# Up products whose right operand holds both parts of the rows side by side, and converted weights made three ahead

## The chip, the core and the metric

The kernel runs on one core of one Trainium2 chip. The metric is the device time of one execution in microseconds (us). The core has a matrix engine (TensorE, PE in the profile, with its weight loads listed apart as PEld), three engines for elementwise work (VectorE or DVE, ScalarE or ACT, GpSimd or POOL), a queue engine (SyncE or SP) and 16 DMA engines. Each engine works through its own list of instructions in the order of the program. Where an instruction needs something of another engine it waits for a semaphore, and what stands behind it on its engine waits too.

## The reference

One decoder block over 512 rows of 2048 channels: RWKV-7 time mixing and sliding-window attention side by side, merged by gates, and then a gated feed-forward part. All values are float32. The change lies in the feed-forward part:

```python
def conv_ffn(h, w_up, conv_w, conv_b, w_down):
    u = h @ w_up                       # (512, 2048) @ (2048, 11264)
    up = jnp.pad(u, ((0, 0), (CONV_W - 1, 0), (0, 0)))
    c = up[:, 0:S] * conv_w[0] + up[:, 1:S + 1] * conv_w[1] + up[:, 2:S + 2] * conv_w[2] + conv_b
    val, gate = jnp.split(c, 2, axis=-1)
    return (jax.nn.silu(gate) * val) @ w_down
```

`h` is the block's state after an RMS norm. `u` is 512 rows by 2 x 5632 columns, the value half and the gate half.

## The kernel before

**Parts.** TensorE multiplies operands of type float32r. To keep the precision of float32, each factor is split into a high part (`hi`, the value rounded to float32r) and a low part (`lo`, what is left). A product is then the sum of three: high weights by high rows, high weights by low rows, low weights by high rows. ScalarE makes the high part with a copy (`act.activation(hi, t, AF.Copy)`), and VectorE makes the low part with a subtraction that reads the high part, so the low part always comes second.

**Stages.** The program runs through the input projection, time mixing, attention and the branch projection (to about 1315 us), the output projection (stage "o", line 997, to about 1470 us), the up projection (line 1133, 1472 to 2374 us) and the down projection (stage "dn", line 997 again, to the end).

**The up stage.** There are 44 blocks `f`, each of 128 value columns and the 128 gate columns that go with them. A block is multiplied by a scheme of seven products in place of eight: the two halves of the contraction, the two halves of the rows (256 each, `TH`) and the two column halves make 2 x 2 matrices, and the sums and differences of the factors are multiplied. The products are named P1, P2, P7, P6, P5, Q4 and P3. The row factors (`b11`, `b21`, `b22`, `t1` to `t4`) are made once, each as two tiles for the high and the low part (`bq`). The weight factors come from memory, some of them with a sum that a DMA forms on the way (`s1`, `s3`), and P6 and P3 need one more sum on VectorE (`sums`, line 1109), which adds in place to the tile that P1 used.

A product is 8 steps `k` of the contraction, and a step is three matmuls of 256 columns (lines 1130 to 1134): `(whi, xh)`, `(whi, xl)`, `(wlo, xh)`. From block 7 on the order within a block is P7, P6, P2, P5, P1 of the next block, Q4, P3. P1, P6, P5 and P3 add up in one PSUM tile X, P7 and Q4 in a tile Y, P2 in a tile Z. Each of these tiles is a whole bank of 512 columns, of which only the left 256 are used.

**Order of the work around a product.** `run(i)` (line 1261) first calls `prep(i + 2)`, then the matmuls `mm`, then `out`, which moves results into the row buffer `u`. `prep(j)` (line 1246) makes the converted weights of step `j`: the sum on VectorE if the product is P6 or P3, then one piece of the convolution of an earlier block (`some_later(1)`), then the high part on ScalarE (line 1114) and the low part on VectorE (line 1116). Nearly every instruction of this stage is held in program order (`pin`). The converted weights `whi` and `wlo` have three buffers each (`hlD`, line 962).

**The convolution** of a block is queued after its P3 and taken piece by piece, one for each `prep`. Piece 0: ScalarE scales the gate half (line 1182), VectorE adds the next tap (line 1185). Piece 1: VectorE adds the last tap, ScalarE applies silu to it (line 1188). Pieces 2 and 3 do the same with the value half, without silu. Piece 4 multiplies the two halves on VectorE (line 1190). Pieces 5 and 6, in odd blocks alone, form the sums that the down stage needs (lines 893 to 897), and the results go out from ScalarE's queue when piece 0 of the next block is taken.

**Results into `u`** (`out`, lines 1157 to 1165): for P1, P6, P5 and P3 ScalarE copies X into a part of `u` (line 1161). For P5, VectorE then adds Y (line 1163), and for P2 and Q4 VectorE adds Z or Y (line 1165). That is three VectorE additions of 128 x 256 in a block.

Of the kernel before, what the change touches and what calls it, by code (L numbers as in the profile page):

```python
# [18 lines left out]
P = 128  # L19
S = 512  # L20
# [114 lines left out]
def block_kernel(ctx: ExitStack, tc: tile.TileContext, d: Dims, a: dict, out: bass.AP):  # L135
    nc = tc.nc
    act, dve, pool, pe, sync = nc.scalar, nc.vector, nc.gpsimd, nc.tensor, nc.sync
# [17 lines left out]
    NPRE = 4  # L155
# [725 lines left out]
    KH = NK // 2  # L881
# [134 lines left out]

    upx = ExitStack()
    bqp = upx.enter_context(tc.tile_pool(name="bqA", bufs=1, reuse_waits="tile"))
    bq = {n: [bqp.tile([P, KH, TH], F32R, name=f"{n}{i}") for i in range(2)] for n in ("b11", "b21")}
    hp = hps.enter_context(tc.tile_pool(name="hhlO", bufs=3, reuse_waits="tile"))  # L1020
    NCC = d.D // S
    ssp = tcp.tile([P, NT, NCC], F32, name="ssp")
# [49 lines left out]
            else:  # L1072
                put(act.activation(dst, src, AF.Copy, scale=g))

    def halves(t):
        return t.rearrange("p (a k) s -> p a (k s)", a=2)

    def high(n, q, pin=pin):
        pin(act.activation(halves(bq[n][0]), q, AF.Copy))

    def low(n, q, pin=pin):
        hi, lo = (halves(x) for x in bq[n])
        pin(dve.tensor_tensor(lo, q, hi.bitcast(F32), op=ALU.subtract))

    us = []
    dve.tensor_scalar(cw[:, 0:3, NF:], cw[:, 0:3, NF:], -1.0, None, op0=ALU.mult)

    class Block:

        def __init__(self, f):
            self.f, self.w, self.hl = f, {}, {}
            self.apart = 2 <= f < NPRE

        def load(self, n):
            f, w = self.f, self.w
# [20 lines left out]
        def mm(self, n):  # L1118
            if n == "P1":
                x = ups.tile([P, S], F32, name="X", tag="X")  # L1120
                self.X = x[:, :TH]
                self.Z = x[:, TH:] if self.f < NPRE else upy.tile([P, S], F32, name="Z", tag="Y")[:, :TH]
            if n == "P7":
                self.Y = upy.tile([P, S], F32, name="Y", tag="Y")[:, :TH]
# [4 lines left out]
            xh, xl = bq[{"P1": "b11", "P2": "b21", "P7": "t3", "P6": "t2", "P5": "t1", "Q4": "t4", "P3": "b22"}[n]]  # L1129
            for k in range(KH):  # L1130
                last = k == KH - 1
                for i, (l, r) in enumerate(((whi, xh), (whi, xl), (wlo, xh))):
                    pin(pe.matmul(ps, l[:, k], r[:, k], start=start and k + i == 0, stop=last and i == 2,  # L1133
                                  skip_group_check=True))

        def out(self, n):
# [8 lines left out]
            if self.f < NPRE:  # L1145
# [3 lines left out]
                if self.apart and n != "P1":  # L1149
                    if n != "P6":  # L1150
# [3 lines left out]
                        for ps in more:  # L1154
# [2 lines left out]
            i, j, ps, first = {"P1": (0, 0, X, True), "P2": (0, 0, Z, False), "P6": (1, 0, X, True), "P5": (1, 1, X, True),  # L1157
                               "Q4": (1, 0, Y, False), "P3": (0, 1, X, True)}[n]
            u = us[self.f % 2][:, i, 2 + j * TH : 2 + (j + 1) * TH]
            if first:  # L1160
                pin(act.activation(u, ps, AF.Copy))  # L1161
                if n == "P5":
                    pin(dve.tensor_tensor(u, u, Y, op=ALU.add))
            else:
                pin(dve.tensor_tensor(u, u, ps, op=ALU.add))

        def place(self):
            pin(act.activation(us[self.f % 2][:, 0, 2 : 2 + TH], self.t1, AF.Copy))
# [137 lines left out]


    bqp = upx.enter_context(tc.tile_pool(name="bqB", bufs=1, reuse_waits="tile"))
    bq.update({n: [bqp.tile([P, KH, TH], F32R, name=f"{n}{i}") for i in range(2)] for n in ("b22", "t1", "t3", "t2", "t4")})
# [183 lines left out]
```

## Time and profile before

| | |
|---|---|
| median of 3 runs | 2803.97 us (2802.36 to 2803.97) |
| profiled execution, its own time | 2801.0 us |
| span of the instructions in it | 2799.2 us |
| up stage in it | 1472 to 2374 us |
| granted TensorE clock, mean | 0.999 |
| DMA over the span | 221 GB/s |

The profile is of one execution. The span runs from its first to its last instruction, and 1.8 us of the execution's own time lie outside it. Engines overlap, so shares of busy time do not add up; what sets the end has to be followed through the waits.

### The profile page before, as it was taken

Reading aid. Unit: us, or ns where it says so; the run is one execution under the profiler, and the core shown is the slowest. Engines: PE = TensorE matmul, PEld = TensorE weight load, DVE = VectorE, ACT = ScalarE, POOL = GpSimd, SP = SyncE. Lnnn points to the kernel's source line nnn. Section 1 sums busy time; section 2 is a strip of 40 time slices with the busy share of each in tenths; the row PEclk is TensorE's granted clock in tenths of the full one; section 3 lists DMA queues with packets and bytes.
Section 4 is the critical chain, followed back from the end, with each engine's and each line's share of the span. In section 5 each row is a group of like instructions: output and inputs, shape, how many; then the busy total and the mean of one; then the engine's idle time right before and its main releaser. Section 6 shows DMA issues by size and latency. Waiting matters only on the chain.

```text
span 2799.2 us, 45969 instructions
## 1 busy us (share of the span) xinstructions
PE 2755.7 (98%) x17466; PEld 2401.1 (86%) x17466; DVE 1985.3 (71%) x3452; ACT 1352.1 (48%) x2278; POOL 231.3 (8%) x307
## 2 busy tenths in 40 slices
PE   6999999999999999999999999999999999999999
PEld 5777788888878788888889999999999999888887
DVE  5588677877787774545678778787777778655555
ACT  4355445545544553322466554545555555444444
POOL 0001110110101001011000011101110101000000
PEclk9999999999999999999999999999999999999999
DMA  7865887777777777888776888888888888877775
GB/s 220 229 159 155 210 208 190 194 193 189 197 182 199 186 177 219 239 255 284 248 254 187 234 230 221 241 233 227 229 242 229 225 232 236 317 243 241 256 256 188
DMA packets 227182, 619.62 MB, mean 221 GB/s; under 512 B 24832, under 2 KB 44944, under 8 KB 225936
## 3 DMA queue, kind: packets, MB, share of 16 engines
q1 hardware_dynamic: 158400, 441.03, 48.2%
q0 software_dynamic: 37216, 136.33, 25.5%
q10 hardware_dynamic: 31344, 39.31, 4.0%
q8 instruction: 137, 2.24, 0.3%
q14 instruction: 85, 0.70, 0.1%
HBM read 566.96 MB, written 191.18 MB: 271 GB/s over the span
## 4 chain that ended last, share of the span: by engine, by line
PE 88%; DVE 6%; ACT 2%; issue 1%; DMA 1%; ACTq 0%; SPq 0%; DVEq 0%
PE X L1133 17%; PE X L997 11%; PE acc L271 10%; PE acc L270 10%; PE acc L269 10%; PE Y L997 9%; PE Y L1133 8%; PE Z L1133 4%; PE psS L766 1%; PE psG L757 1%; PE bulk L697 1%; DVE wlo L1116 1%; PE bulk L745 1%; ACT whi L1114 1%; PE psU L760 1%
## 5 line engine op out<-in xcount | busy, mean ns | idle before, releaser
L270 PE MATMUL acc<-xlo,whi 128*128 128x512 f32 x1152 | 461.8, 401 | 0.0
L269 PE MATMUL acc<-xhi,whi 128*128 128x512 f32 x1152 | 459.5, 399 | 1.9 <-DVE xlo L315 1.9
L271 PE MATMUL acc<-xhi,wlo 128*128 128x512 f32 x1152 | 460.7, 400 | 0.3 <-DVE wlo L255 0.3
L254 ACT ACTIVATE whi<-raw 128x512 fp32r<-128x512 f32 x352 | 219.8, 629 | 394.5 <-PE acc L270 298.6
L990 DVE TENSOR_TENSOR wlo<-raw,whi 128x1024 fp32r<-128x1024 f32 x210 | 256.9, 1224 | 199.3 <-ACT whi L989 198.2
L989 ACT ACTIVATE whi<-raw 128x1024 fp32r<-128x1024 f32 x210 | 222.6, 1060 | 282.8 <-PE X L997 147.1
L255 DVE TENSOR_TENSOR wlo<-raw,whi 128x512 fp32r<-128x512 f32 x352 | 240.9, 688 | 151.2 <-ACT whi L254 136.5
L1116 DVE TENSOR_TENSOR wlo<-raw,whi 128x1024 fp32r<-128x1024 f32 x184 | 224.6, 1222 | 77.2 <-ACT whi L1114 77.0
L1133 PE MATMUL X<-b,whi 128*128 128x256 f32 x1472 | 268.9, 283 | 0.2 <-ACT whi L1114 0.2
L1133 PE MATMUL X<-t,whi 128*128 128x256 f32 x1408 | 257.2, 283 | 1.4 <-ACT u L1161 1.4
L1133 PE MATMUL Y<-t,whi 128*128 128x256 f32 x1408 | 257.1, 283 | 0.0
L269 PEld LDWEIGHTS acc<-xhi,whi 128*128 128x128 f32 x1152 | 217.0, 188 | 42.7 <-DVE xlo L315 2.2
L270 PEld LDWEIGHTS acc<-xlo,whi 128*128 128x128 f32 x1152 | 216.9, 188 | 41.8 <-issue 2.0
L271 PEld LDWEIGHTS acc<-xhi,wlo 128*128 128x128 f32 x1152 | 217.0, 188 | 39.4 <-issue 0.9
L1133 PEld LDWEIGHTS X<-b,whi 128*128 128x128 f32 x1472 | 229.6, 192 | 0.4 <-ACT whi L1114 0.4
L1114 ACT ACTIVATE whi<-a 128x1024 fp32r<-128x1024 f32 x124 | 130.9, 1056 | 201.8 <-DVE a L1109 196.4
L1133 PEld LDWEIGHTS X<-t,whi 128*128 128x128 f32 x1408 | 219.6, 192 | 1.6 <-ACT u L1161 1.6
L1133 PEld LDWEIGHTS Y<-t,whi 128*128 128x128 f32 x1408 | 219.6, 192 | 0.0
L1133 PE MATMUL X<-b,wlo 128*128 128x256 f32 x736 | 208.6, 283 | 0.9 <-DVE wlo L1116 0.9
L1114 ACT ACTIVATE whi<-raw 128x1024 fp32r<-128x1024 f32 x184 | 192.9, 1049 | 22.7 <-ACT whi L1114 14.7
L1133 PE MATMUL X<-t,wlo 128*128 128x256 f32 x704 | 199.6, 283 | 0.7 <-DVE wlo L1116 0.7
L1116 DVE TENSOR_TENSOR wlo<-a,whi 128x1024 fp32r<-128x1024 f32 x124 | 151.9, 1225 | 67.5 <-ACT whi L1114 66.9
(387 smaller groups left out, 5795.7 us busy)
## 6 DMA issues: line engine op xcount, KB each, us to landing
raw<-in_w_up_dram SPq DMA_DIRECT2D x170, 512.0 KB
raw<-in_w_z_dram SPq DMA_DIRECT2D x288, 256.0 KB
s_dn<-in_w_dn_dram POOLq DMA_DIRECT2D x88, 512.0 KB, 7.2
raw<-s_dn SPq DMA_DIRECT2D x88, 512.0 KB
raw<-in_w_up_dram POOLq DMA_DIRECT2D x80, 512.0 KB, 8.5
raw<-in_w_dn_dram SPq DMA_DIRECT2D x66, 512.0 KB
s_dn<-in_w_dn_dram SPq DMA_DIRECT2D x44, 512.0 KB
s_dn<-s_dn SPq DMA_DIRECT2D x44, 512.0 KB
```

Source lines behind the costliest of these rows:

```text
L254: act.activation(hi, raw, AF.Copy)
L255: dve.tensor_tensor(lo, raw, hi.bitcast(F32), op=ALU.subtract)
L269: stream.append(pe.matmul(acc, whi[:, j], xhi[:, k], start=first, stop=False))
L270: stream.append(pe.matmul(acc, whi[:, j], xlo[:, k], start=False, stop=False))
L271: stream.append(pe.matmul(acc, wlo[:, j], xhi[:, k], start=False, stop=last))
L697: ins = pe.matmul(ps[:, n], wt[:, 0, n], both(n), start=True, stop=False)
L989: act.activation(whi, wr, AF.Copy)
L990: dve.tensor_tensor(wlo, wr, whi.bitcast(F32), op=ALU.subtract)
L997: pe.matmul(dst, l[:, q, ts], r[:, es], start=fst and j == 0, stop=lst and j == 2, skip_group_check=True)
L1114: pin(act.activation(hi, t, AF.Copy))
L1116: return lambda: pin(dve.tensor_tensor(lo, t, hi.bitcast(F32), op=ALU.subtract))
L1133: pin(pe.matmul(ps, l[:, k], r[:, k], start=start and k + i == 0, stop=last and i == 2, skip_group_check=True))
```

## The change

Three things are changed.

1. The two parts of each row factor lie in one tile of shape 128 x 8 x 2 x 256, so that for a step `k` the high and the low part stand next to each other. In blocks 7 to 42, for the five products P7, Q4, P2, P5 and P3, one matmul of 512 columns multiplies `whi[k]` by both parts, and one of 256 columns multiplies `wlo[k]` by the high part. The wide matmul puts high by high into the left half of the PSUM tile and high by low into the right half. P1 and P6 keep their three matmuls, as do all products of blocks 0 to 6 and 43.
2. The right halves have to be added as well. `out` issues five further VectorE additions of 128 x 256 in such a block: one for P2, two for P5, one for Q4, one for P3.
3. The converted weights have four buffers, and from step 48 on they are made three products ahead (`prep(i + 3)`). Step 48 itself calls `prep` twice. The scratch for the descriptors of GpSimd's DMAs is set to 8192 bytes.

```diff
-    hlp = ctx.enter_context(tc.tile_pool(name="hlD", bufs=3, reuse_waits="tile"))
+    hlp = ctx.enter_context(tc.tile_pool(name="hlD", bufs=4, reuse_waits="tile"))
...
-    bq = {n: [bqp.tile([P, KH, TH], F32R, name=f"{n}{i}") for i in range(2)] for n in ("b11", "b21")}
+    bqt = {n: bqp.tile([P, KH, 2, TH], F32R, name=n) for n in ("b11", "b21")}
+    bq = {n: [t[:, :, i] for i in range(2)] for n, t in bqt.items()}
...
+    WIDE = ("P7", "Q4", "P2", "P5", "P3")
...
+            self.wide = WIDE if NPRE + 3 <= f < NF - 1 else ()
...
+                if n in self.wide:
+                    pin(pe.matmul(self.full[into], whi[:, k], bqt[nm][:, k].rearrange("p e s -> p (e s)"),
+                                  start=start and k == 0, stop=False, skip_group_check=True))
+                    pin(pe.matmul(ps, wlo[:, k], xh[:, k], start=False, stop=last, skip_group_check=True))
+                    continue
...
+            adds = [Y] if n == "P5" else []
+            adds += [self.full["Y"][:, TH:]] if n in ("P5", "Q4") and "P7" in self.wide else []
+            adds += [self.full["Z"][:, TH:]] if n == "P2" and n in self.wide else []
+            adds += [self.full["X"][:, TH:]] if n in ("P5", "P3") and n in self.wide else []
             if first:
                 pin(act.activation(u, ps, AF.Copy))
-                if n == "P5":
-                    pin(dve.tensor_tensor(u, u, Y, op=ALU.add))
             else:
-                pin(dve.tensor_tensor(u, u, ps, op=ALU.add))
+                adds.insert(0, ps)
+            for more in adds:
+                pin(dve.tensor_tensor(u, u, more, op=ALU.add))
...
+    AHEAD = 12 * NPRE
...
         if i > 4 * NPRE + 2:
-            prep(i + 2, 2 if 24 <= i <= 8 * NPRE else 1)
+            if i <= AHEAD:
+                prep(i + 2, 2 if 24 <= i <= 8 * NPRE else 1)
+            if i >= AHEAD:
+                prep(i + 3)
...
-    nc = _bacc.Bacc("TRN2", target_bir_lowering=False, num_devices=1)
+    nc = _bacc.Bacc("TRN2", target_bir_lowering=False, num_devices=1, dynamic_dma_scratch_size=8192)
```

Here is TensorE at the end of a P7 and the start of the P6 behind it, before. `t_15095` and `t_15096` are the high and the low part of P7's row factor, `t_15097` and `t_15098` those of P6.

```order
L1133 MATMUL Y<-t_15095,whi 128x256
L1133 MATMUL Y<-t_15096,whi 128x256
L1133 MATMUL Y<-t_15095,wlo 128x256
L1133 MATMUL X<-t_15097,whi 128x256
L1133 MATMUL X<-t_15098,whi 128x256
L1133 MATMUL X<-t_15097,wlo 128x256
```

And in the changed kernel, the end of P7 of block 7, and the start of P6.

```order
L1143 MATMUL Y<-t_15091,wlo 128x256
L1141 MATMUL Y<-t_15091,whi 128x512
L1143 MATMUL Y<-t_15091,wlo 128x256
L1146 MATMUL X<-t_15092,whi 128x256 x2
L1146 MATMUL X<-t_15092,wlo 128x256
```

Two matmuls stand where there were three in each step of P7, and P6 is as it was.

Next is VectorE in the middle of a block, from the addition of Z (P2) to the conversion behind that of Q4, before. L1116 makes a low part, L1109 is the sum for P6 or P3, L1185 adds a tap and L1190 multiplies the halves.

```order
L1165 TENSOR_TENSOR u_15589<-u_15589,Z 128x256
L1185 SCALAR_TENSOR_TENSOR c_24484<-u_15587,par,c_24484 128x512
L1116 TENSOR_TENSOR wlo<-raw,whi 128x1024
L1163 TENSOR_TENSOR u_15589<-u_15589,Y 128x256
L1109 TENSOR_TENSOR a_24083<-a_24083,raw 128x1024
L1190 TENSOR_TENSOR c_24484<-c_24484,c_24419 128x512
L1116 TENSOR_TENSOR wlo<-a_24083,whi 128x1024
L1116 TENSOR_TENSOR wlo<-raw,whi 128x1024
L1165 TENSOR_TENSOR u_15589<-u_15589,Y 128x256
L1109 TENSOR_TENSOR a_24314<-a_24314,raw 128x1024
L1116 TENSOR_TENSOR wlo<-a_24314,whi 128x1024
```

The same stretch in the changed kernel (L1120 is the low part, L1113 the sum, L1182 every addition into `u`, L1202 a tap, L1207 the multiplication).

```order
L1182 TENSOR_TENSOR u_15582<-u_15582,Z 128x256 x2
L1113 TENSOR_TENSOR a_22984<-a_22984,raw 128x1024
L1202 SCALAR_TENSOR_TENSOR c_23353<-u_15580,par,c_23353 128x512
L1120 TENSOR_TENSOR wlo<-a_22984,whi 128x1024
L1182 TENSOR_TENSOR u_15582<-u_15582,Y 128x256 x2
L1182 TENSOR_TENSOR u_15582<-u_15582,X 128x256
L1207 TENSOR_TENSOR c_23353<-c_23353,c_23296 128x512
L1120 TENSOR_TENSOR wlo<-raw,whi 128x1024
L1113 TENSOR_TENSOR a_23180<-a_23180,raw 128x1024
L1120 TENSOR_TENSOR wlo<-a_23180,whi 128x1024
L1182 TENSOR_TENSOR u_15582<-u_15582,Y 128x256 x2
L1120 TENSOR_TENSOR wlo<-raw,whi 128x1024
```

The additions are doubled and the one of X is new. The sum for P6 now stands ahead of the last tap (L1202) instead of ahead of the multiplication, which has come to stand after the additions of P5; the conversions and sums are all one product earlier with respect to the additions.

More of the change, by code (lines that the diff above doesn't have):

```diff
@@ L1073, in transposed, with by_channel @@
                 put(act.activation(dst, src, AF.Copy, scale=g))
-    def halves(t):
-        return t.rearrange("p (a k) s -> p a (k s)", a=2)
+    def by_channel(q):
+        return q.rearrange("p a (k s) -> p (a k) s", s=TH)
     def high(n, q, pin=pin):
-        pin(act.activation(halves(bq[n][0]), q, AF.Copy))
+        pin(act.activation(bq[n][0], by_channel(q), AF.Copy))
     def low(n, q, pin=pin):
-        hi, lo = (halves(x) for x in bq[n])
-        pin(dve.tensor_tensor(lo, q, hi.bitcast(F32), op=ALU.subtract))
+        hi, lo = bq[n]
+        pin(dve.tensor_tensor(lo, by_channel(q), hi.bitcast(F32), op=ALU.subtract))
     us = []
     dve.tensor_scalar(cw[:, 0:3, NF:], cw[:, 0:3, NF:], -1.0, None, op0=ALU.mult)
+    WIDE = ("P7", "Q4", "P2", "P5", "P3")
     class Block:
         def __init__(self, f):
-            self.f, self.w, self.hl = f, {}, {}
+            self.f, self.w, self.hl, self.full = f, {}, {}, {}
             self.apart = 2 <= f < NPRE
+            self.wide = WIDE if NPRE + 3 <= f < NF - 1 else ()
         def load(self, n):
@@ L1120, in mm @@
                 x = ups.tile([P, S], F32, name="X", tag="X")
+                z = x if self.f < NPRE else upy.tile([P, S], F32, name="Z", tag="Y")
                 self.X = x[:, :TH]
-                self.Z = x[:, TH:] if self.f < NPRE else upy.tile([P, S], F32, name="Z", tag="Y")[:, :TH]
+                self.Z = x[:, TH:] if self.f < NPRE else z[:, :TH]
+                self.full.update(X=x, Z=z)
             if n == "P7":
-                self.Y = upy.tile([P, S], F32, name="Y", tag="Y")[:, :TH]
+                self.full["Y"] = upy.tile([P, S], F32, name="Y", tag="Y")
+                self.Y = self.full["Y"][:, :TH]
             into = {"P2": "Z", "P7": "Y", "Q4": "Y"}.get(n, "X")
@@ L1128, in mm @@
             whi, wlo = (x.rearrange("p (k c) -> p k c", c=P) for x in self.hl.pop(n))
-            xh, xl = bq[{"P1": "b11", "P2": "b21", "P7": "t3", "P6": "t2", "P5": "t1", "Q4": "t4", "P3": "b22"}[n]]
+            nm = {"P1": "b11", "P2": "b21", "P7": "t3", "P6": "t2", "P5": "t1", "Q4": "t4", "P3": "b22"}[n]
+            xh, xl = bq[nm]
             for k in range(KH):
                 last = k == KH - 1
+                if n in self.wide:
[3 more added lines that the diff above has]
+                    continue
                 for i, (l, r) in enumerate(((whi, xh), (whi, xl), (wlo, xh))):
@@ L1308, in block_kernel @@
     bqp = upx.enter_context(tc.tile_pool(name="bqB", bufs=1, reuse_waits="tile"))
-    bq.update({n: [bqp.tile([P, KH, TH], F32R, name=f"{n}{i}") for i in range(2)] for n in ("b22", "t1", "t3", "t2", "t4")})
+    bqt.update({n: bqp.tile([P, KH, 2, TH], F32R, name=n) for n in ("b22", "t1", "t3", "t2", "t4")})
+    bq.update({n: [t[:, :, i] for i in range(2)] for n, t in bqt.items()})
     up = upx.enter_context(tc.tile_pool(name="upw", bufs=1, side="left", reuse_waits="tile"))
```

## The prediction

> **What bounds the kernel now.** I read the page's chain of waits first, then the up stage, 1472 to 2374 us, alone, because the change lies in it.
>
> ```profile
> PE 88%; DVE 6%; ACT 2%; issue 1%; DMA 1%; ACTq 0%; SPq 0%; DVEq 0%
> ```
>
> This is the chain that ended last, by engine: TensorE is the bound of most stages. The table by stretch says how that is in the steady part of the up stage and in the down stage; its columns are length, then busy time and count for PE, PEld, DVE, ACT and POOL, then clock, DMA share and GB/s.
>
> ```profile
> 1700.00:2370.00 670.00, 669.55 (x5578) 669.14 (x5577) 526.78 (x632) 341.62 (x465) 69.86 (x81) 1.00 0.85 231
> 2374.00:2799.00 425.00, 419.66 (x1851) 346.75 (x1850) 253.62 (x266) 201.94 (x231) 2.14 (x4) 1.00 0.75 251
> ```
>
> TensorE is busy for 669.55 of 670 us. The matmuls overlap in the records, so their price is the distance from start to start, which the timeline gives: 256 columns wide in the up stage, 512 wide in the down stage.
>
> ```profile
> 1899.81 0.28 PE L1133 MATMUL Z<-b,wlo 128*128 128x256 f32 x1
> ...
> 1900.17 0.28 PE L1133 MATMUL Z<-b,wlo 128*128 128x256 f32 x1
> ...
> 2500.10 0.39 PE L997 MATMUL X<-whi,hhi 128*128 128x512 f32 x1
> ...
> 2500.78 0.39 PE L997 MATMUL X<-whi,hhi 128*128 128x512 f32 x1
> ```
>
> From one `wlo` to the next lie three matmuls and 0.36 us, so a narrow one takes 120.0 ns. Three wide ones take 0.68 us, 226.7 ns each. A product of 24 narrow matmuls takes 2.88 us and a block of seven 20.16 us, and there is nothing to spare in it: 670 us are 33.2 blocks.
>
> VectorE is busy for 526.78 of the 670 us, 79%, 15.85 us in a block. It looks as if 4.3 us were free in each block. What its idle time waits for is in the table of waits of VectorE, 1700 to 2370 us (total, times, longest):
>
> ```profile
> DVE wlo L1116 <- ACT whi L1114: 109.5, 146, 1.6
> DVE c L1185 <- ACT c L1182: 17.2, 17, 1.9
> DVE u L1163 <- ACT u L1161: 12.9, 17, 0.8
> DVE u L1165 <- PE Y L1133: 0.2, 1, 0.2
> ```
>
> VectorE as good as never waits for TensorE (0.2 us), and through ScalarE's copy of X for 12.9 us, 0.39 us a block. 109.5 us, 3.30 a block, are waits for the high part of weights that ScalarE is just making. So the idle time is mostly not slack: VectorE hands something to ScalarE and needs the answer. The timeline of VectorE through one odd block (all of that engine's rows, start and duration, in brackets the idle time ahead) shows where:
>
> ```profile
> 1897.81 1.23 DVE L1116 TENSOR_TENSOR wlo<-raw,whi 128x1024 fp32r<-128x1024 f32 x1 [1.64 <-ACT whi L1114]
> 1899.09 0.75 DVE L1185 SCALAR_TENSOR_TENSOR c<-u,par,c 128x512 f32<-128x512 f32 x1
> 1900.04 1.23 DVE L1116 TENSOR_TENSOR wlo<-a,whi 128x1024 fp32r<-128x1024 f32 x1 [0.20 <-ACT whi L1114]
> 1901.18 0.41 DVE L1165 TENSOR_TENSOR u<-u,Z 128x256 f32<-128x256 f32 x1
> 1901.51 0.74 DVE L1185 SCALAR_TENSOR_TENSOR c<-u,par,c 128x512 f32<-128x512 f32 x1
> 1902.17 1.22 DVE L1116 TENSOR_TENSOR wlo<-raw,whi 128x1024 fp32r<-128x1024 f32 x1
> 1904.15 0.42 DVE L1163 TENSOR_TENSOR u<-u,Y 128x256 f32<-128x256 f32 x1 [0.76 <-ACT u L1161]
> 1904.48 1.22 DVE L1109 TENSOR_TENSOR a<-a,raw 128x1024 f32<-128x1024 f32 x1
> 1905.62 0.68 DVE L1190 TENSOR_TENSOR c<-c,c 128x512 f32<-128x512 f32 x1
> 1906.89 1.23 DVE L1116 TENSOR_TENSOR wlo<-a,whi 128x1024 fp32r<-128x1024 f32 x1 [0.58 <-ACT whi L1114]
> 1908.03 0.42 DVE L893 TENSOR_TENSOR tq<-c 128x256 f32<-128x256 f32 x1
> 1908.37 0.42 DVE L894 TENSOR_TENSOR tq<-c,c 128x256 f32<-128x256 f32 x1
> 1908.70 1.22 DVE L1116 TENSOR_TENSOR wlo<-raw,whi 128x1024 fp32r<-128x1024 f32 x1
> 1909.84 0.41 DVE L1165 TENSOR_TENSOR u<-u,Y 128x256 f32<-128x256 f32 x1
> 1910.17 1.22 DVE L1109 TENSOR_TENSOR a<-a,raw 128x1024 f32<-128x1024 f32 x1
> 1911.31 0.41 DVE L896 SCALAR_TENSOR_TENSOR tq<-tq,c 128x256 f32<-128x256 f32 x1
> 1911.75 0.42 DVE L897 SCALAR_TENSOR_TENSOR tq<-tq,c 128x256 f32<-128x256 f32 x1
> 1912.59 1.23 DVE L1116 TENSOR_TENSOR wlo<-a,whi 128x1024 fp32r<-128x1024 f32 x1 [0.41 <-ACT whi L1114]
> 1914.63 0.75 DVE L1185 SCALAR_TENSOR_TENSOR c<-u,par,c 128x512 f32<-128x512 f32 x1 [0.81 <-ACT c L1182]
> 1915.58 1.23 DVE L1116 TENSOR_TENSOR wlo<-raw,whi 128x1024 fp32r<-128x1024 f32 x1 [0.20 <-ACT whi L1114]
> 1916.72 0.74 DVE L1185 SCALAR_TENSOR_TENSOR c<-u,par,c 128x512 f32<-128x512 f32 x1
> 1919.11 1.23 DVE L1116 TENSOR_TENSOR wlo<-raw,whi 128x1024 fp32r<-128x1024 f32 x1 [1.65 <-ACT whi L1114]
> ```
>
> I price this chain from start to start, which counts the small overlap of records correctly. A low part with ready work behind it: 1.14 (1900.04 to 1901.18). **Sum link**, from a sum over ScalarE's conversion of it to its low part: 2.41 (1904.48 to 1906.89), 2.42 with other work between (1910.17 to 1912.59); whatever fits between costs nothing. **Silu link**, from the last gate tap to the next low part, behind silu and a conversion on ScalarE: 2.39 (1916.72 to 1919.11). A tap: 0.66 if what follows is ready (1901.51 to 1902.17), 0.95 if not (1914.63 to 1915.58). An addition: 0.33. L893 and L894: 0.67 together; L896 and L897: 0.44 and about 0.34.
>
> The block adds up to 7 x 1.14 + 2 x 2.41 + 2.39 + taps 0.95 + 0.95 + 0.66 + 3 x 0.33 + 0.67 = 19.41 us. The trace has 21.30, of which 0.76 and 0.81 are the two waits that the list leaves out. 0.3 us remain, so these prices hold to 1.5%. Two blocks are 40.32, so the even one takes 19.02. Without the waits on the copy of X and on the scaling (0.39 + 0.52 us a block by the table of waits) the chain of VectorE and ScalarE needs 19.25 us for 20.16 of TensorE: **the real slack is 0.9 us a block, not 4.3.**
>
> **The change, part by part.** *TensorE.* A merged step saves 3 x 120.0 - (226.7 + 120.0) = 13.3 ns. Five products of 8 steps save 0.53 us, so TensorE's block falls to 19.63 us, and 36 blocks would give 19.2 us if TensorE stayed the bound. Wide and narrow in turn are in no row. At best the step takes 346.7 ns; at worst, if the change of width costs what the merge saves, the old 360. I take 346.7, as each width holds its distance among its own kind. What follows makes the choice matter only for rival A.
>
> The Trainium skill, page "TensorE: Matmul & The Clock Gate", section "Back-to-back issue gap", has N / 2.4 + 2.5 ns for a lone warm matmul. By that rule the merge would save only 2.5 ns a step, 3.6 us in all. The rows disagree with it here (120.0 against 109.2, 226.7 against 215.8), and I keep to the rows.
>
> *VectorE's additions.* P2, P5 (twice) and Q4 get an addition to the part of `u` that the one before it has just written, and P3 gets one behind ScalarE's copy. The price of two that depend on each other, and of the multiplication with ready work behind it, is in earlier blocks:
>
> ```profile
> 1549.96 0.42 DVE L1155 TENSOR_TENSOR u<-u,X 128x256 f32<-128x256 f32 x1 [1.05 <-ACT u L1153]
> 1550.42 0.42 DVE L1155 TENSOR_TENSOR u<-u,Y 128x256 f32<-128x256 f32 x1
> 1550.76 0.68 DVE L1190 TENSOR_TENSOR c<-c,c 128x512 f32<-128x512 f32 x1
> 1551.36 1.22 DVE L1116 TENSOR_TENSOR wlo<-raw,whi 128x1024 fp32r<-128x1024 f32 x1
> ```
>
> So 0.46 for one that is followed by its dependent, 0.34 otherwise. Of the eight additions of a block four are followed by a dependent one: 4 x 0.46 + 4 x 0.33 = 3.16 us, against 0.99 before. That is 2.17 us more into a slack of 0.9.
>
> *Three ahead.* The conversions keep their order on both engines; each merely moves one product ahead of the additions. That widens TensorE's distance from a late low part, but a chain that is slower on average uses up any distance. Sum link and silu link remain, as sum, conversion and low part still stand together in one `prep`, and silu still stands ahead of a conversion. What changes is the filler: the sum for P6 now has the last tap between (0.66, free) and the multiplication outside (0.60); the sum for P3 in odd blocks has L893 and L894 between (free), and L896 and L897 outside (0.78 in two blocks, 0.39 in one).
>
> The new chain of one block: low parts 7 x 1.14 = 7.98; sum links 4.82; silu link 2.39; multiplication 0.60; additions 3.16; L896 and L897 0.39; together 19.34. To this come the first tap of either half, at 0.66 to 0.95: 20.66 to 21.24. I take 0.73 for each, near the lower end, as the new addition of P3 ahead of the first gives ScalarE 0.33 us more to get its scaling done: **20.80 us**. The waits on the scaling and on the copy of X, 0.9 a block before, I take as gone: what they waited for is then long there. TensorE needs 19.63 and waits for the rest. Per block 20.80 - 20.16 = 0.64 us more, 23.0 us in 36 blocks.
>
> *The rest.* At the switch to three ahead one more conversion is made in one product, 1.14 to 2.4 us of the chain, hidden or not by the slack of blocks 4 to 6: 0 to 2.4, I take 1. The fourth buffer also serves stages "o" and "dn"; TensorE idles there for only 425 - 419.66 = 5.3 us, part of it the end of the program, so the bounds are 0 and 5 us gained, and I take 0, as no more weights than before are asked for. The interleaved tiles of row factors change no matmul's length. The smaller scratch for GpSimd's descriptors has no row of its own; GpSimd is busy for 69.86 of 670 us and hands out the same transfers, and a block that gets longer lowers the DMA share of 0.85, so I take 0, with 5 us lost at the outside.
>
> Sum: +23 + 1 = **+24 us**. On the profiled execution that is 2801.0 + 24 = 2825 us (span 2823); the median of the runs shown stands 3 us higher, so 2803.97 + 24 = **2828 us**.
>
> **Rivals.** *A: TensorE stays the bound, faster.* If making weights three ahead let ScalarE finish its high part before VectorE asks, the links would lose their idle time, on average 1.65 + 0.58 in every block and 0.41 or more for the other sum: 2.6 us off 20.80 leaves 18.2, under the 19.63 of TensorE, and 19.2 us are gained: 2785 us. For it: ScalarE is busy for only 341.62 of 670 us and TensorE is at 100%. Against it: both links are dependences in a pinned order that the change leaves. It decides where a block's chain falls under 19.63.
>
> The Trainium skill, page "Perfetto Trace Analysis", section "Identifying the Most-Contended Engine", judges VectorE by its share of busy time. By it 79% plus 2.17 us in a block of 19.63 would make some 92%, TensorE would stay the bound, and A's time would hold. The trace so far speaks against reading it so here, since most of VectorE's idle time waits on ScalarE.
>
> *B: half of that.* If the links lose about 0.6 us a block, the chain ends at 20.16 and the time is the old one, 2804 us. Only the small fillers speak for it.
>
> *C: the waits stay as well.* VectorE waits at the copy of X for P5 now and would do so for P3's new addition too, at 0.76 us as in the block shown: with one such wait in each block the chain takes 21.56, +50 us, 2855 us. Against it: in a chain that is late anyway the product lies three conversions back.
>
> *D: the change doesn't do what it says.* The program's order has the 512-wide matmuls in all 36 blocks and 180 further additions, so this gets no share.
>
> **How the numbers follow.** Forecast 0.74, A 0.13, B 0.06, C 0.07. The forecast's own range: with dependent additions at 0.34 and taps at 0.66 the chain is 20.18 (+1 us), with taps at 0.95 and the remaining 0.3 us of the check it is 21.54 (+50); both at once are unlikely, and I take 20.4 to 21.2, with the switch +10 to +40, or 2814 to 2844. For eight in ten I extend that to B's time below and towards C above: 2803 to 2847, which leaves out A and most of C. A measurement of this kernel can tell 0.2% from no change, 5.6 us. Faster by more: 0.13 (A). Within: 0.08 (B and the forecast's lowest edge). Slower: 0.79.
>
> **What would show it.** TensorE should stop now and then for the low part (L1120), 1.2 us a block in all, of which the records show less since their ends reach 0.16 us past the next start; VectorE's share should rise to about 86%, its waits for the high part staying near 3 us a block, and those on the copy of X and on the scaling going. From one wide matmul to the next in a product it should be 0.347 us. Blocks should take about 41.6 us a pair. If TensorE is still at 100% and a pair takes 39.3 us, A is right and the links were not binding. If VectorE waits for ScalarE's copies of X, C is.

## The result and the profile after

| | before | after |
|---|---|---|
| median | 2803.97 us (5 runs, 2801.38 to 2804.63) | 2831.38 us (5 runs, 2827.83 to 2834.41) |
| ratio of the two, 95% interval | | 1.0102 (1.0091 to 1.0112) |
| profiled execution, its own time | 2801.0 us | 2828.6 us |
| span in it | 2799.2 us | 2826.8 us |
| up stage, first up matmul to first down matmul | 902.0 us | 931.5 us |

The changed kernel is 27.4 us slower by the medians and 27.6 us by the spans of the profiled executions. The up stage alone has grown by 29.5 us; the rest of the program has become 1.9 us shorter. The chain of waits of the changed kernel, by engine:

```profile
PE 73%; DVE 14%; ACT 7%; issue 4%; DMA 1%; ACTq 0%; SPq 0%; DVEq 0%
```

TensorE had 88% of that chain before. VectorE and ScalarE have taken up most of what it lost. In the steady part of the up stage the table by stretch (length, then busy time and count for PE, PEld, DVE, ACT and POOL, then clock, DMA share, GB/s) reads:

```profile
1700.00:2370.00 670.00, 645.00 (x4104) 579.69 (x4103) 564.50 (x770) 329.80 (x450) 69.03 (x80) 1.00 0.83 224
```

TensorE is busy for 645 us of 670, where it had 669.55. VectorE is busy for 84%, and not for 100%. What it waits for in these 670 us is one line of the table of waits (total, times, longest):

```profile
DVE wlo L1120 <- ACT whi L1118: 97.2, 97, 1.6
```

The waits on ScalarE's copy of X and on its scaling, 30.1 us before, are gone. The waits for the high part are still there, 3.03 us a block (32.06 blocks of 20.90 us in the window) against 3.30. TensorE's own waits in the same stretch:

```profile
PE Y L1141 <- DVE u L1182: 25.0, 32, 1.4
```

TensorE stops once in each block, at the first matmul of Q4, which writes to Y, because VectorE is still adding Y of P5 to `u`. VectorE through one pair of blocks (start, duration, in brackets the idle time ahead; "x2" is two instructions):

```profile
1901.14 1.23 DVE L1120 TENSOR_TENSOR wlo<-a,whi 128x1024 fp32r<-128x1024 f32 x1 [1.13 <-ACT whi L1118]
1902.29 0.87 DVE L1182 TENSOR_TENSOR u<-u,Y 128x256 f32<-128x256 f32 x2
1903.07 1.22 DVE L1120 TENSOR_TENSOR wlo<-raw,whi 128x1024 fp32r<-128x1024 f32 x1
1904.21 0.41 DVE L1182 TENSOR_TENSOR u<-u,X 128x256 f32<-128x256 f32 x1
1904.54 0.74 DVE L1202 SCALAR_TENSOR_TENSOR c<-u,par,c 128x512 f32<-128x512 f32 x1
1905.20 1.22 DVE L1120 TENSOR_TENSOR wlo<-raw,whi 128x1024 fp32r<-128x1024 f32 x1
1906.34 0.75 DVE L1202 SCALAR_TENSOR_TENSOR c<-u,par,c 128x512 f32<-128x512 f32 x1
1908.73 1.23 DVE L1120 TENSOR_TENSOR wlo<-a,whi 128x1024 fp32r<-128x1024 f32 x1 [1.65 <-ACT whi L1118]
1909.87 0.75 DVE L1202 SCALAR_TENSOR_TENSOR c<-u,par,c 128x512 f32<-128x512 f32 x1
1910.65 1.23 DVE L1120 TENSOR_TENSOR wlo<-raw,whi 128x1024 fp32r<-128x1024 f32 x1
1911.80 0.87 DVE L1182 TENSOR_TENSOR u<-u,Z 128x256 f32<-128x256 f32 x2
1912.58 1.22 DVE L1113 TENSOR_TENSOR a<-a,raw 128x1024 f32<-128x1024 f32 x1
1913.72 0.75 DVE L1202 SCALAR_TENSOR_TENSOR c<-u,par,c 128x512 f32<-128x512 f32 x1
1915.01 1.23 DVE L1120 TENSOR_TENSOR wlo<-a,whi 128x1024 fp32r<-128x1024 f32 x1 [0.54 <-ACT whi L1118]
1916.15 0.87 DVE L1182 TENSOR_TENSOR u<-u,Y 128x256 f32<-128x256 f32 x2
1917.12 0.42 DVE L1182 TENSOR_TENSOR u<-u,X 128x256 f32<-128x256 f32 x1
1917.46 0.69 DVE L1207 TENSOR_TENSOR c<-c,c 128x512 f32<-128x512 f32 x1
1918.06 1.22 DVE L1120 TENSOR_TENSOR wlo<-raw,whi 128x1024 fp32r<-128x1024 f32 x1
1919.20 1.22 DVE L1113 TENSOR_TENSOR a<-a,raw 128x1024 f32<-128x1024 f32 x1
...
1921.55 1.23 DVE L1120 TENSOR_TENSOR wlo<-a,whi 128x1024 fp32r<-128x1024 f32 x1 [0.46 <-ACT whi L1118]
...
1925.74 0.75 DVE L1202 SCALAR_TENSOR_TENSOR c<-u,par,c 128x512 f32<-128x512 f32 x1
1926.60 1.22 DVE L1120 TENSOR_TENSOR wlo<-raw,whi 128x1024 fp32r<-128x1024 f32 x1
...
1942.94 1.23 DVE L1120 TENSOR_TENSOR wlo<-a,whi 128x1024 fp32r<-128x1024 f32 x1 [1.13 <-ACT whi L1118]
```

A pair takes 41.80 us (1901.14 to 1942.94), 20.90 a block, where it took 40.32. In the rows shown VectorE is as good as never idle except ahead of the low part of a sum (1.13, 0.54 and 0.46) and behind silu (1.65): in each of these places it has itself just handed ScalarE the input that ScalarE converts. TensorE at the end of P1 and the start of Q4, and then in steps of the next P7, which also writes to Y:

```profile
1916.61 0.28 PE L1146 MATMUL X<-b,wlo 128*128 128x256 f32 x1
1917.16 0.47 PE L1141 MATMUL Y<-t,whi 128*128 128x512 f32 x1 [0.28 <-DVE u L1182]
...
1923.25 0.40 PE L1141 MATMUL Y<-t,whi 128*128 128x512 f32 x1
...
1925.01 0.40 PE L1141 MATMUL Y<-t,whi 128*128 128x512 f32 x1
```

Q4 starts at 1917.16, as soon as the two additions of Y that began at 1916.15 are over. From 1923.25 to 1925.01 lie five merged steps of a wide and a narrow matmul, 0.352 us each, against 0.360 for three narrow ones.

### The profile page after: what moved, and what is told of

It is laid out like the page before. It is cut to its first block, busy times and chain, and to the rows that moved or that the text cites. A ratio compares the mean times of both kernels' runs of the same rounds, so it can differ in the third digit from the quotient of the medians.

```text
span 2826.8 us, 43359 instructions
## 1 busy us (share of the span) xinstructions
PE 2754.0 (97%) x16026; PEld 2327.5 (82%) x16026; DVE 2048.4 (72%) x3632; ACT 1348.9 (48%) x2278; POOL 231.3 (8%) x307
## 4 chain that ended last, share of the span: by engine, by line
PE 73%; DVE 14%; ACT 7%; issue 4%; DMA 1%; ACTq 0%; SPq 0%; DVEq 0%
PE X L997 11%; PE acc L271 10%; PE acc L270 10%; PE acc L269 10%; PE Y L997 9%; ACT whi L1118 5%; DVE wlo L1120 4%; PE X L1146 4%; PE Y L1141 3%; PE X L1141 2%; DVE u L1182 2%; DVE a L1113 2%; PE Y L1143 1%; PE Z L1141 1%; PE X L1143 1%
## 5 line engine op out<-in xcount | busy, mean ns | idle before, releaser
L1141 PE MATMUL Y<-t,whi 128*128 128x512 f32 x576 | 209.0, 403 | 29.3 <-DVE u L1182 29.3
L1120 DVE TENSOR_TENSOR wlo<-a,whi 128x1024 fp32r<-128x1024 f32 x124 | 152.0, 1225 | 118.1 <-ACT whi L1118 118.1
L1120 DVE TENSOR_TENSOR wlo<-raw,whi 128x1024 fp32r<-128x1024 f32 x184 | 224.5, 1222 | 15.6 <-ACT whi L1118 12.5
L997 PE MATMUL X<-whi,hhi 128*128 128x512 f32 x480 | 187.3, 390 | 0.7 <-ACT u L1178 0.7
L997 PE MATMUL X<-wlo,hhi 128*128 128x512 f32 x480 | 187.1, 390 | 0.0
L997 PE MATMUL X<-whi,hlo 128*128 128x512 f32 x480 | 187.0, 390 | 0.0
L1146 PE MATMUL X<-b,whi 128*128 128x256 f32 x896 | 163.8, 284 | 0.2 <-ACT whi L1118 0.2
L1143 PE MATMUL Y<-t,wlo 128*128 128x256 f32 x576 | 162.0, 281 | 0.0
L1141 PEld LDWEIGHTS Y<-t,whi 128*128 128x128 f32 x576 | 108.2, 188 | 60.5 <-ACT u L1178 27.4
L1146 PE MATMUL X<-t,whi 128*128 128x256 f32 x832 | 151.8, 283 | 1.4 <-ACT u L1178 1.4
```

Source lines behind the costliest of these rows:

```text
L997: pe.matmul(dst, l[:, q, ts], r[:, es], start=fst and j == 0, stop=lst and j == 2, skip_group_check=True)
L1120: return lambda: pin(dve.tensor_tensor(lo, t, hi.bitcast(F32), op=ALU.subtract))
L1141: pin(pe.matmul(self.full[into], whi[:, k], bqt[nm][:, k].rearrange("p e s -> p (e s)"), start=start and k == 0, stop=False, skip_group_ch ...
```

## Experiments

My theory: VectorE and ScalarE form one chain, in which two sum links and one silu link leave VectorE idle in every block; five additions make that chain longer than TensorE's block. The main rival: making weights three ahead, or the wide matmul itself, costs the time. Times are medians with the ratio to the kernel before, run beside them on the same chip (2801.29 to 2802.95 us).

### The additions left out

```diff
             adds = [Y] if n == "P5" else []
-            adds += [self.full["Y"][:, TH:]] if n in ("P5", "Q4") and "P7" in self.wide else []
-            adds += [self.full["Z"][:, TH:]] if n == "P2" and n in self.wide else []
-            adds += [self.full["X"][:, TH:]] if n in ("P5", "P3") and n in self.wide else []
```

The right halves (high weights by low rows of the five products) are computed but not added.

> The changed kernel without the five further additions of VectorE per block; the right halves (high weights by low rows of five products) are left out of the result. Theory (the chain of VectorE and ScalarE sets the pace because of the additions): the chain falls under TensorE's block, TensorE is the bound again at 20.16 us less 40 merged steps, whose distance in the changed kernel's trace is 0.353 us instead of 0.360, so 19.88 us a block, 10 us less in 36 blocks, with 2 to 3 us given back at the switch to three ahead: 2794 to 2798 us. VectorE's idle time will again end with ScalarE's copies or TensorE. Rival 1 (the wide matmuls are what costs): 2820 us or more, as they all stay. Rival 2 (three ahead, four buffers or the smaller scratch cost it): 2820 us or more.

Measured: 2801.91 us, ratio 0.9996 (0.9987 to 1.0006). That is 4 us above the range that I expected. The steady block takes 20.01 us, the up stage 898.7. The table by stretch, and the waits of VectorE in the same 670 us:

```profile
1700.00:2370.00 670.00, 668.01 (x4304) 603.93 (x4304) 528.47 (x639) 346.47 (x470) 70.08 (x81) 1.00 0.87 233
```

```profile
DVE wlo L1120 <- ACT whi L1118: 110.0, 151, 1.7
DVE c L1199 <- ACT c L1196: 31.7, 33, 1.6
```

TensorE is nearly full again (668.01), VectorE waits for the scaling again, and all of the loss is gone, with the wide matmuls and three ahead still in place. So the five additions cost what the change costs. But the gain that the merge had promised, 19 us, did not appear either. From the start of one P2 to the next it takes 19.88 us and about 20.13 in turn, so something still holds TensorE in every second block. The next two runs take the look-ahead and the merge apart.

### Only the look-ahead, and the wide matmuls split

The first of these keeps buffers, three ahead, scratch and the tiles with both parts, but multiplies all products by three narrow matmuls, without the further additions.

```diff
-            self.wide = WIDE if NPRE + 3 <= f < NF - 1 else ()
+            self.wide = ()
```

> Four buffers, three ahead, the interleaved row factors and the smaller scratch, but no wide matmul and no further addition. Theory: TensorE stays the bound at 20.16 us a block, and only the switch to three ahead costs something: 2803 to 2807 us. Rival 2 (these parts carry the loss): 2815 to 2831 us.

Measured: 2808.83 us, ratio 1.0020 (1.0011 to 1.0029), up stage 908.3 us. So this part by itself costs 6.5 us, which I had not expected (2803 to 2807 us). Where: the two stretches of the up stage in the kernel before and in this one.

```profile
1560.00:1700.00 140.00, 136.14 (x1121) 134.71 (x1120) 110.95 (x140) 72.53 (x101) 14.68 (x17) 1.00 0.84 228
```

```profile
1560.00:1700.00 140.00, 134.07 (x1098) 132.04 (x1097) 109.34 (x134) 71.89 (x99) 14.72 (x17) 1.00 0.84 225
1700.00:2370.00 670.00, 669.02 (x5559) 667.58 (x5558) 521.50 (x631) 341.98 (x462) 70.07 (x81) 1.00 0.86 230
```

Around the switch (it lies between 1560 and 1700 us) 23 matmuls fewer are done, 2.8 us at 120.0 ns. In the steady part 5559 stand against 5578, 2.3 us. (The busy time shows less, since the records of matmuls overlap.) From the start of one P2 to the next, the block at the switch takes 22.15 us where it took 20.16.

The second splits each wide matmul into two of 256 columns, into either half, with all additions.

```diff
-                    pin(pe.matmul(self.full[into], whi[:, k], bqt[nm][:, k].rearrange("p e s -> p (e s)"),
-                                  start=start and k == 0, stop=False, skip_group_check=True))
+                    for e, r in enumerate((xh, xl)):
+                        pin(pe.matmul(self.full[into][:, e * TH : (e + 1) * TH], whi[:, k], r[:, k],
+                                      start=start and k + e == 0, stop=False, skip_group_check=True))
```

> As the changed kernel with all its additions, but each wide matmul is written as two of 256 columns, one into either half of the PSUM tile. TensorE has its old block of 20.16 us. Theory: the chain sets 20.85 us a block whatever TensorE needs below that, so the time is that of the changed kernel, 2827 to 2835 us, and TensorE idles less. Rival 1 (the wide matmuls are what costs): 2804 to 2808 us. If TensorE's time and the additions both counted in part, about 2838.

Measured: 2833.5 us, ratio 1.0111 (1.0095 to 1.0126), block 20.91 us. The width of the matmul makes no difference that can be seen while the chain of VectorE and ScalarE is the bound. TensorE, with more work of its own, merely waits less at the same place (25.0 us with the merge), here in its table of waits, 1700 to 2370 us:

```profile
PE Y L1142 <- DVE u L1183: 17.5, 16, 1.7
```

### Two products wide

```diff
-    WIDE = ("P7", "Q4", "P2", "P5", "P3")
+    WIDE = ("P2", "P3")
```

Only P2 and P3 are merged here, with one addition more for each.

> Wide matmuls for P2 and P3 alone, so three further additions in a block (P2, P5's reading of X's right half is left in only where the product is wide, P3), by the code two: P2 and P3. Theory: two additions are 0.46 + 0.33 = 0.8 us on a chain of 19.25, 20.05 us at the most, still under TensorE's 20.16 less 16 x 7 ns = 20.05: no loss except at the switch, 2800 to 2808 us. Rival 3 (every addition costs its share wherever the chain stands): two fifths of the loss, 2813 to 2816 us.

Measured: 2811.21 us, ratio 1.0033 (1.0020 to 1.0045), block 20.38 us. This met no theory well. By prices the chain should still have had room, and the time should have come under 2808; by a cost in proportion to the additions it should have been near 2813. The theory left out what the look-ahead costs alone: by the medians this kernel is 2.4 us above that one (2808.83), with overlapping intervals, and by the up stages of the profiled executions 4.8 us (913.1 against 908.3). TensorE waits 7.6 us for P5's additions here, in 16 of the 33 blocks, so every second block is already over the edge while the other is not. A limit on the mean of two blocks does not show that; the two would have to be reckoned apart, which is not done here.

### The links loosened, with all additions kept

If the links are the cause, the loss must go when VectorE makes its sums earlier. Here, from block 7 on, the sum for P6 is made behind the conversion one product ahead of its own, and that for P3 two products ahead.

```diff
+    EARLY = 12 * NPRE + 4
+    SOONER = {'P6': 1, 'P3': 2}
...
             lo = B[f].parts(nm)
             if not split:
                 lo()
+            if i >= EARLY:
+                for k, (g, q) in enumerate(steps[i : i + 4]):
+                    if k and i + k > EARLY and (k == SOONER.get(q) or i == EARLY and k < SOONER.get(q, 0)):
+                        B[g].sums(q)
```

> The changed kernel, with the sum for P6 made one product ahead of its conversion and that for P3 two, so that ScalarE has its operand before VectorE wants the answer. Nothing else is changed, all five additions stay. Theory (VectorE's idle time at the links is what the additions ran into): the two sum links lose 0.54 and, on average, 0.80 us of idle time, the chain falls from 20.90 to 19.56 us a block. What then ends last is a second path, from the end of P3 over ScalarE's copy of X, the scaling, the taps and P5's additions to the start of Q4, about 20.4 us: 2811 to 2818 us. Rival (VectorE is simply too busy with additions; its idle time is no cause): 2829 to 2834 us.

Measured: 2803.88 us, ratio 1.0001 (0.9992 to 1.0010), block 20.14 us. That is better than I expected (20.4 us). VectorE's waits, 1700 to 2370 us:

```profile
DVE wlo L1120 <- ACT whi L1118: 82.0, 69, 1.6
DVE c L1202 <- ACT c L1199: 2.1, 1, 2.1
```

97 waits for the high part have become 69, so one link of three, P3's, is gone; P6's sum and silu remain. VectorE's rows for P6, from the low part of P7 on:

```profile
1909.97 1.22 DVE L1120 TENSOR_TENSOR wlo<-raw,whi 128x1024 fp32r<-128x1024 f32 x1
1911.11 1.22 DVE L1113 TENSOR_TENSOR a<-a,raw 128x1024 f32<-128x1024 f32 x1
...
1913.45 1.23 DVE L1120 TENSOR_TENSOR wlo<-a,whi 128x1024 fp32r<-128x1024 f32 x1 [0.46 <-ACT whi L1118]
```

The changed kernel has the same rows at the same distances (1918.06, 1919.20, 1921.55): nothing of VectorE's stands between P7's low part and P6's sum, so moving this sum by one product moves nothing, and the gain is that of P3's sum alone. No run makes P6's sum sooner than that. In the changed kernel's rows above, P3's low part at 1915.01 comes 2.43 us after its sum at 1912.58; with sum and tap apart it needs 1.14 + 0.66 = 1.80, which saves 0.63. The sum now also stands ahead of the first tap of the value half, which therefore follows at 0.66 and not at 0.78, and this 0.12 I had left out. Together 0.75, and the block fell by 0.76.

The next one also moves silu: the piece with the last gate tap is emitted behind the conversion of the same `prep` on ScalarE, and no longer ahead of it.

```diff
-            some_later(1)
+            later_first = i <= EARLY or not later or later[0].part not in (1,)
+            if later_first:
+                some_later(1)
             lo = B[f].parts(nm)
+            if not later_first:
+                some_later(1)
```

> As the run with the sums earlier, and silu stands behind the conversion of that product on ScalarE instead of ahead of it, so that the silu link of 2.39 us loses its 1.65 us of idle time too. Theory: chain about 17.9 us, second path under 19.9, TensorE the bound at 20.16 less 40 x 6.7 ns = 19.89 us a block; 9.6 us less than before, of which the switch to three ahead gives back 3 to 6: 2796 to 2802 us, VectorE still with all its additions. Rival (VectorE is simply too busy): 2829 to 2834 us.

Measured: 2791.99 us, ratio 0.9965 (0.9952 to 0.9979), block 19.88 us. I had expected 2796 to 2802 us. With all eight additions in it this kernel is 11 us faster than the one before. Its table by stretch, and three rows of VectorE:

```profile
1700.00:2370.00 670.00, 668.58 (x4324) 606.51 (x4324) 594.92 (x810) 355.87 (x476) 72.05 (x85) 1.00 0.87 236
```

```profile
1912.06 0.75 DVE L1202 SCALAR_TENSOR_TENSOR c<-u,par,c 128x512 f32<-128x512 f32 x1
1912.72 1.22 DVE L1120 TENSOR_TENSOR wlo<-a,whi 128x1024 fp32r<-128x1024 f32 x1
1913.86 1.22 DVE L1113 TENSOR_TENSOR a<-a,raw 128x1024 f32<-128x1024 f32 x1
```

From the last gate tap to the next low part it is 0.66 us, where it was 2.39 (1906.34 to 1908.73 in the changed kernel). VectorE is busy for 594.92 us, 89%, more than in the changed kernel (84%), and TensorE is full. VectorE was never short of time; it was short of work that it was allowed to do.

The control gives the kernel before the same two moves, with no merge, no additions and two ahead.

> The kernel before with the same two moves (sums earlier, silu behind the conversion), nothing else. Theory: TensorE is the bound at 20.16 us a block with and without the links: 2800 to 2806 us. Rival (the moves are a gain of their own, so the run above says nothing on the additions): under 2795 us.

Measured: 2799.58 us, ratio 0.9992 (0.9983 to 1.0001), block 20.16 us. Loosening the links by itself gives nothing that can be told from no change, since TensorE was the bound there.

### Two ahead

The change as it is, with four buffers, but with weights made two ahead throughout.

```diff
-    AHEAD = 12 * NPRE
+    AHEAD = 10**6
```

> The changed kernel with its wide matmuls and additions, but converted weights two ahead as before (four buffers stay). Theory: a chain that is slower than TensorE does not care how far ahead it may run: 2826 to 2834 us. Rival (three ahead costs the 6 us it costs alone here as well): 2821 to 2826 us. Rival (three ahead is needed to hide the additions): over 2838 us.

Measured: 2827.91 us, ratio 1.0092 (1.0078 to 1.0105), block 20.92 us. The look-ahead doesn't matter for the length of a block that the chain sets; what it moves is the place where TensorE stops. TensorE's waits, 1700 to 2370 us:

```profile
PE X L1143 <- DVE wlo L1120: 17.5, 32, 0.8
PE X L1146 <- DVE wlo L1120: 3.7, 16, 0.3
```

With two ahead it stops for the low part, as I had forecast for three ahead; with three ahead the weights are there, and the additions are late.

The same edit in the kernel with loosened links:

> Sums and silu moved as in the last run of that kind, all wide matmuls and additions, but weights made two ahead. Theory: TensorE is the bound at 19.88 us a block here too, and the additions of P5 no longer stand behind a sum in VectorE's list, so what three ahead cost at the switch comes back: 2786 to 2791 us. Rival (three ahead is needed once the chain is near TensorE's pace): 2795 us or more.

Measured: 2788.34 us, ratio 0.9953 (0.9941 to 0.9966), block about 19.87 us. The ratio lies 0.0012 under that of three ahead, but the intervals overlap, so no gain is claimed.

### What three ahead costs by itself

The kernel with the look-ahead only lost 6.5 us without any further addition. My explanation: three ahead puts P3's sum and its link, 2.4 us, ahead of the additions of P5 on VectorE, and Q4 may not write Y before these have read it. In that kernel's own table of waits TensorE shows this wait only twice, 1700 to 2370 us:

```profile
PE Y L1146 <- DVE u L1182: 1.0, 2, 0.6
```

Shorter waits can hide in the overlap of the records, so this run alone does not show the cause. If the explanation holds, moving P3's sum alone (two products earlier, all else as in that kernel) must take the loss away.

> Three ahead alone, without wide matmuls and further additions, and the sum for P3 made two products ahead of its conversion. Theory (three ahead alone costs because P5's addition of Y, for which Q4 waits, stands behind P3's sum link, 1.3 us longer than a plain conversion): with the link's wait gone the steady block falls from 20.23 to 20.16 us and TensorE no longer waits at Q4; 2 to 3 us less than three ahead alone, 2803 to 2807 us. Rival (the loss lies in the buffers, the smaller scratch or the interleaved row factors): 2807 to 2811 us, blocks still 20.23.

Measured: 2802.04 us, ratio 1.0003 (0.9994 to 1.0012). The loss is gone, and the time is 1 us under the range that I expected. The same two stretches as above:

```profile
1560.00:1700.00 140.00, 135.51 (x1110) 133.52 (x1109) 112.11 (x141) 72.45 (x101) 14.69 (x17) 1.00 0.85 229
1700.00:2370.00 670.00, 669.98 (x5583) 669.74 (x5582) 516.69 (x632) 348.45 (x466) 69.88 (x81) 1.00 0.86 232
```

5583 matmuls in the steady part where there were 5559. Of the 23 matmuls missing around the switch 12 are back, and the block at the switch takes 21.42 us against 22.15; this execution started its up stage 6 us later than the other, so the count there is less certain.

### All seven products wide

With the links loosened and two ahead, P1 and P6 are merged too, which makes ten additions in a block.

```diff
-    WIDE = ("P7", "Q4", "P2", "P5", "P3")
+    WIDE = ("P7", "Q4", "P2", "P5", "P3", "P1", "P6")
...
-            adds += [self.full["X"][:, TH:]] if n in ("P5", "P3") and n in self.wide else []
+            adds += [self.full["X"][:, TH:]] if n in ("P1", "P6", "P5", "P3") and n in self.wide else []
```

> Sums and silu moved, two ahead, and all seven products wide (P1 and P6 as well), with two additions more in a block, ten in all. Theory: the chain grows by 0.33 + 0.33 to about 0.9 us, from 17.9 to at most 18.8, and stays under TensorE, whose block falls by 16 x 6.7 ns to 19.78: 36 x 0.107 = 4 us less than with five wide products, 2782 to 2788 us. Rival (VectorE is full: 15.85 + 2.17 + 0.9 = 18.9 us busy in 19.8, waits come on top): 2795 us or more.

Measured: 2782.53 us, ratio 0.9936 (0.9923 to 0.9950), block about 19.77 us. It is the best of all versions run.

```profile
1700.00:2370.00 670.00, 668.50 (x3830) 582.02 (x3829) 617.58 (x880) 350.92 (x478) 72.04 (x85) 1.00 0.87 240
```

VectorE is now busy for 92% and TensorE is still full. VectorE is idle for 52 us of 670, so there is little room for more work on it.

## Why the prediction was right

The forecast was 2828 us and the time 2831. By its steps:

- **TensorE to VectorE and ScalarE as the bound: right, and shown.** Without the additions the loss is gone; without the merge it stays; with the links loosened and all additions kept it turns into a gain. The real slack, not the idle time, decided.
- **The additions: right.** In the rows after: Q4's pair 0.78, P3's one 0.33, P2's pair 0.78, P5's three 0.97 + 0.34. That is 3.20 us against 3.16.
- **The links and the fillers: right.** 2.43 for P3's sum, 2.34 and 2.35 for P6's and 2.39 for silu, against 2.41, 2.41 and 2.39. In naming the tiles I made a slip: the sum with the last tap behind it is P3's, and the one after it, behind which L893 and L894 stand in odd blocks, is P6's of the next block, not the other way round. The section on the change has the same slip. I had priced both alike, so no number of the forecast hangs on it.
- **The waits on the scaling and on the copy of X: right.** They are gone, which rules out rival C. Waits for the high part are 3.03 us a block, "near 3", and VectorE's share is 84% against 86%.
- **The block: 20.90 us against 20.80.** The first tap of the gate half came at 0.66 in the one block of the pair and at 0.86 in the other, that of the value half at 0.78 in both, a mean of 0.77 against 0.73. Two of these and the additions make 0.12 more, and P6's shorter link takes off some 0.06, which leaves the difference to within 0.05. 0.74 x 36 = 26.6 us, where I had 23.0.
- **The switch and three ahead: too small.** 29.5 - 26.6 = 2.9 us against 1. The look-ahead alone costs 6.5 us, 2.8 of them around the switch. The step that failed is "That widens TensorE's distance from a late low part": it does, but I did not ask which other instructions fall behind P3's sum on VectorE. P5's additions do, and Q4 waits for them. In the change at most 2.9 us of the 6.5 show. That the rest is hidden where the chain sets the pace anyway fits the run with two ahead (1.0092 against 1.0102, with overlapping intervals), but is not shown by itself.
- **Where TensorE stops: wrong for the same reason.** It waits at the start of Q4 for P5's additions and not for the low part, 20.90 - 19.89 = 1.0 us a block where I had 1.2; the records show 25.0 us in 32 blocks, 0.8.
- **The merged step: too good.** I took 346.7 ns and the rows have 352 to 353, a saving of about 7 ns and not 13.3. TensorE's block is then 2 x 2.88 + 40 x 0.3533 = 19.89 us and not 19.63, and the kernel with loosened links, where TensorE is full, shows it: 19.88. This left the forecast alone, since TensorE was not the bound, but rival A would have had 0.27 x 36 = 9.7 us, 2794 us, and not 2785.
- **The rest: right within the noise.** Outside the up stage 1.9 us were gained where I took 0. That is within what executions differ by: outside the up stage it was 1897.2 us before and 1895.3 after, but 1894.9 in the kernel before with its links loosened, and 1901.8 in the changed kernel without additions. That these 1.9 us just offset the 1.9 us by which the switch came out above the forecast is luck; the error of 3.6 us that is left is the block's.

By the rule for a lone matmul in the Trainium skill, page "TensorE: Matmul & The Clock Gate", section "Back-to-back issue gap", the merge would have saved an estimated 2.5 ns a step. The rows show about 7, so neither that rule nor my taking each width at its own distance gave the step's price. The Trainium skill, page "Perfetto Trace Analysis", section "Identifying the Most-Contended Engine", goes by the share of busy time for VectorE. By it the kernel with VectorE at 89% should be nearer to a VectorE bound than the one at 84%. It was the other way round: the one at 84% was bound by VectorE's and ScalarE's chain, the ones at 89% and 92% by TensorE.

## What to carry to other kernels

Idle time of an engine that hands work to a second one and needs its answer next is no slack: add up the distances from start to start around such a block, hand-overs included, and compare that sum with the bound engine's block. Before work is put on such an engine, take the hand-overs apart: make the operand some steps before its conversion, and place the activation behind the conversion that is needed sooner. When a step is moved ahead, list what falls behind it on its engine, and look for a write to a PSUM tile that waits for a read among it.

## What was not expected of the hardware

A wide and a narrow matmul in turn run at one of two distances. In the kernel with all seven products wide the timeline of TensorE has both (the first and the last wide matmul of two stretches in which it never stops):

```profile
1881.62 0.39 PE L1141 MATMUL X<-b,whi 128*128 128x512 f32 x1
...
1911.78 0.39 PE L1141 MATMUL Z<-b,whi 128*128 128x512 f32 x1
...
1919.67 0.40 PE L1141 MATMUL Y<-t,whi 128*128 128x512 f32 x1
...
1949.71 0.40 PE L1141 MATMUL Z<-b,whi 128*128 128x512 f32 x1
```

87 steps in 30.16 us are 346.7 ns each, exactly the sum of the two distances that I had taken; 85 steps in 30.04 us are 353.4. Between the two stretches two steps took 0.51 and 0.42 us, so TensorE had stopped for a moment, and in this execution the distance changes almost only where TensorE stops. The changed kernel runs almost throughout at the longer one. What sets it is open; no run here was made for it. If it could be held at the shorter one, 40 steps of 6.7 ns in 36 blocks would be worth 9.6 us by estimate.
